# The last output projection of two attention layers, taken by token tiles instead of by weight pieces

## The chip, the cores and the metric

The kernel runs on one core of a Trainium2 chip. The engines of the core work side by side, each through its own instructions in order: TensorE (PE) multiplies matrices and transposes by multiplying with an identity, VectorE (DVE), ScalarE (ACT) and GpSimd (POOL) do the elementwise work, and SyncE (SP) issues the transfers (DMAs) between the chip's memory and the on-chip memory. The metric is the time of one execution in device microseconds (us), as the median of several runs.

## The reference

The model takes 512 tokens of width 1024. Two attention layers (the second one is a retention layer) are followed by a gated delta net and a mixture of experts. Cut to what matters here:

```python
def first_block(x, mem, norm_g, ..., w_out, final_norm_g):
    mem_n = rmsnorm(mem, mem_norm_g)
    for i in range(2):
        h = rmsnorm(x, norm_g[i])
        proj = h @ w_in[i]                     # q, k, v, q_mem, z
        main = fox_attention(...) if i == 0 else retention(...)   # 12 heads of 128
        memo = mem_cross_attention(q_mem, mem_n, w_mem_kv[i])     # 4 heads of 128
        o = concatenate([main, memo], -1) * silu(z)
        x = x + o @ w_out[i]                   # 2048 x 1024, the output projection
    return rmsnorm(x, final_norm_g)
...
# then: x -> rms_norm(x, mix_norm_g_2) @ w_in_2 -> short convolution + gated delta net (4 heads)
# beta = sigmoid(b), g = -exp(a_log) * softplus(a + dt_bias); b and a are 8 of the 3592 columns of w_in_2
# -> output projection, mixture of 32 experts
```

## The kernel before

Every matrix product is made in three matmuls, since each float32 operand is kept as a high and a low part (`wh`/`wl` for weights, `hH`/`hL` for the normalized tokens, `oh`/`ol` for an attention head's gated output). A weight piece is a DMA of 512 KB into a buffer `raw`; ACT writes `wh` from it (L201) and DVE writes `wl` = `raw` - `wh` (L202). There are two weight pools, each with its own `raw` and `wh`/`wl` buffers; `piece` (L187) takes them in a fixed rotation unless it is told a pool.

Tokens lie in four tiles of 128 (t = 0 to 3). A layer's output projection is made in three parts as the heads come; `out_proj` (L737) is called for the last six heads with `steps`, the parts of the normalization that follows. Its weight is cut in two column halves (nh) and three row pieces (kq), six pieces in all, and 4 x 6 x 6 = 144 matmuls of 128x512. Before the change each half goes piece by piece over all four tiles; only in the second half are the second and third piece kept, so that one tile after the other is finished. `add` (L753) puts each sum on the token rows `x`; `steps[0]` then does the squares, the product with the gain `gb` on POOL and, after the second half, the reciprocal square root and the scaling of the rows (`xs` in layer 1, `x` in layer 2). When all four tiles are finished, `steps[1]` transposes each tile on PE (8 transposes of 128x128, outputs `trp` or `att`) and ACT and DVE split the transposed tile into `hH` and `hL`. Only then can the next layer's projections run on that tile.

Layer 1 is followed by retention (`ret`): its first pair's projection goes tile by tile (`proj_tok`). Layer 2 is followed by the delta net (`dn`). It starts with `proj_few`, a narrow projection whose 8 columns `ba` give beta and the gate; it is made in two halves of 256 tokens, as are the k, q and v projections of head 0. From `ba` a chain runs over several engines: four small transposes on PE, a softplus and a running sum, a transfer out and back (`gd`, then `gb`, broadcast to all partitions), the decay `dtmp` and `E` on DVE, another pair of transfers (`lda`, `la`), a triangular inverse on DVE (`lx`), and its result goes into matmuls on PE through `XX`.

The instructions of each engine stand in an order which a scheduler made from the program text when the kernel was built; at run time each engine keeps that order and waits on semaphores. SP issues the DMAs in such an order too, so that a DMA that waits for a free buffer holds back the ones behind it.

## Time and profile before

| | |
|---|---|
| Time, median of 3 runs | 1806.19 us (1806.1 to 1808.04) |
| The profiled execution | 1808.52 us |
| Span from its first to its last instruction | 1806.7 us |
| PE busy | 1744.4 us, 97% |
| DVE, ACT, POOL busy | 56%, 32%, 8% |
| Mean granted PE clock | 0.991 of full speed |
| Last out_proj of layer 1 | its PE work begins at 523 us and ends at 559 us |
| Last out_proj of layer 2 | ends at 975 us |
| Delta net | from 986 us to about 1290 us |

Times inside the profile count from the span's start. A row of the timeline gives the start, the duration and, in brackets, how long the engine stood idle before it and what ended that. PE is pipelined: its rows overlap, and what a matmul costs is the distance to the next start. The table of stretches gives busy times and PEclk, the granted clock as a share of 2.4 GHz, so that 0.50 is 1.2 GHz.

### The profile page before, as it was taken

The page shows a single profiled execution, that of the slowest core. Times are in us where ns is not written, and L with a number is a line of the kernel's source. Part 1 is how long each engine was busy: PE and PEld are TensorE (multiplying, and loading weights), DVE is VectorE, ACT ScalarE, POOL GpSimd, SP SyncE. Part 2 cuts the span into 40 slices and gives each one's busy share as a digit, 9 for nine tenths or more (in the row PEclk, how much of TensorE's full clock was granted, in tenths as well). Part 3 has the DMA queues.
Part 4 walks back from the last instruction along what each step waited for, and adds up shares of the span by engine and source line. Part 5 has one row for each costly group of instructions (what it writes and reads, how often), then busy time and mean ns, then how long its engine had stood idle before and what let it go on. Part 6 is the DMA issues. An engine that isn't in the chain of part 4 may idle for free.

```text
span 1806.7 us, 25586 instructions
## 1 busy us (share of the span) xinstructions
PE 1744.4 (97%) x9945; PEld 1294.4 (72%) x9945; DVE 1016.6 (56%) x2557; ACT 576.8 (32%) x1082; POOL 146.7 (8%) x170
## 2 busy tenths in 40 slices
PE   6999999999998999999997999999999999999996
PEld 6888888878888998999876877778743544454443
DVE  7654563663756445454566788875454435444534
ACT  5543332443444232222344534434311111111112
POOL 1000000000004110111004000001200000000001
PEclk9999999999999999999998999999999999999998
DMA  7733233223232222223322243326699999999981
GB/s 235 198 95 90 76 93 94 82 82 94 59 120 86 82 71 82 83 72 92 90 77 56 78 98 83 89 66 243 265 422 390 408 406 422 407 411 408 420 332 48
DMA packets 199149, 320.94 MB, mean 178 GB/s; under 512 B 18189, under 2 KB 158950, under 8 KB 174322
## 3 DMA queue, kind: packets, MB, share of 16 engines
q1 hardware_dynamic: 199026, 319.28, 50.0%
q8 instruction: 79, 1.29, 0.3%
q14 instruction: 44, 0.36, 0.1%
HBM read 314.24 MB, written 5.01 MB: 177 GB/s over the span
## 4 chain that ended last, share of the span: by engine, by line
PE 86%; DVE 8%; DMA 2%; ACT 1%; issue 1%; POOL 0%; SPq 0%; POOLq 0%; DVEq 0%; ACTq 0%
PE acc L142 47%; PE pg L223 12%; PE att L142 7%; PE att L223 7%; PE pd L223 6%; PE trp L147 3%; PE trp L223 1%; PE trp L142 1%; DVE wl L202 1%; DVE rst L172 1%; DVE rsr L181 1%; DMA la<-lda 1%; DMA raw<-in_w_mem_kv_dram 0%; DVE on L1009 0%; DVE rss L1007 0%
## 5 line engine op out<-in xcount | busy, mean ns | idle before, releaser
L202 DVE TENSOR_TENSOR wl<-raw,wh 128x1024 fp32r<-128x1024 f32 x184 | 227.5, 1238 | 259.0 <-ACT wh L201 252.3
L201 ACT ACTIVATE wh<-raw 128x1024 fp32r<-128x1024 f32 x184 | 194.4, 1057 | 350.9 <-PE acc L142 327.9
L142 PE MATMUL acc<-hH,wh 128*128 128x512 f32 (+1 forms) x760 | 300.2, 396 | 0.0
L142 PE MATMUL acc<-hL,wh 128*128 128x512 f32 (+1 forms) x760 | 300.1, 395 | 0.0
L142 PE MATMUL acc<-hH,wl 128*128 128x512 f32 (+1 forms) x760 | 299.3, 394 | 0.0
L223 PE MATMUL pg<-mw,mhT 128*64 128x512 f32 x1024 | 230.3, 597 | 0.0
L142 PE MATMUL acc<-wh,hH 128*128 128x256 f32 x576 | 162.0, 281 | 4.2 <-ACT hH L236 4.2
L142 PEld LDWEIGHTS acc<-hH,wl 128*128 128x128 f32 x760 | 143.2, 188 | 27.3
L142 PEld LDWEIGHTS acc<-hH,wh 128*128 128x128 f32 x760 | 143.3, 189 | 26.9
L142 PEld LDWEIGHTS acc<-hL,wh 128*128 128x128 f32 x760 | 143.2, 188 | 26.7
L223 PEld LDWEIGHTS pg<-mw,mhT 128*64 128x64 f32 x1024 | 69.3, 137 | 129.8 <-issue 129.7
L142 PE MATMUL acc<-wh,hL 128*128 128x256 f32 x576 | 161.4, 280 | 0.0
L142 PE MATMUL acc<-wl,hH 128*128 128x256 f32 x576 | 161.3, 280 | 0.0
L142 PE MATMUL acc<-wh,oh 128*128 128x512 f32 x320 | 126.4, 395 | 1.4 <-ACT oh L236 1.4
L142 PE MATMUL acc<-wl,oh 128*128 128x512 f32 x320 | 126.0, 394 | 0.0
L142 PE MATMUL acc<-wh,ol 128*128 128x512 f32 x320 | 125.2, 392 | 0.0
L223 PE MATMUL pd<-mw,h 128*64 128x512 f32 (+1 forms) x544 | 118.3, 577 | 3.0 <-DVE h L1743 3.0
L142 PEld LDWEIGHTS acc<-wh,hH 128*128 128x128 f32 x576 | 108.6, 189 | 5.0 <-ACT hH L236 4.7
L142 PEld LDWEIGHTS acc<-wl,hH 128*128 128x128 f32 x576 | 108.7, 189 | 0.4
L142 PEld LDWEIGHTS acc<-wh,hL 128*128 128x128 f32 x576 | 108.5, 189 | 0.0
L1724 ACT ACTIVATE gu<-pg,gt 128x512 f32<-128x512 f32 x32 | 22.0, 688 | 267.0 <-PE pg L223 253.1
L1783 DVE TENSOR_TENSOR yl<-pd,yh 128x512 fp32r<-128x512 f32 x30 | 19.3, 686 | 137.3 <-ACT yh L1782 137.3
(536 smaller groups left out, 2900.0 us busy)
## 6 DMA issues: line engine op xcount, KB each, us to landing
mw<-in_w_gate_dram SPq DMA_DIRECT2D x64, 1024.0 KB, 10.7
mw<-in_w_up_dram SPq DMA_DIRECT2D x64, 1024.0 KB, 10.3
mw<-in_w_down_dram SPq DMA_DIRECT2D x62, 1024.0 KB, 10.5
raw<-in_fox_w_in_dram SPq DMA_DIRECT2D x56, 512.0 KB, 3.9
raw<-in_w_out_dram SPq DMA_DIRECT2D x40, 512.0 KB, 3.7
raw<-in_ret_w_in_dram SPq DMA_DIRECT2D x32, 512.0 KB, 3.9
raw<-in_w_in_dram SPq DMA_DIRECT2D x28, 512.0 KB, 4.0
raw<-in_w_mem_kv_dram SPq DMA_DIRECT2D x16, 512.0 KB, 8.5
```

Source lines behind the costliest of these rows:

```text
L142: self.pe.matmul(o, l, r, start=start, stop=stop)
L147: self.pe.transpose(o, i, self.ident[b:b + n, b:b + n])
L172: yield V.scalar_tensor_tensor(out=t, in0=r, scalar=w, in1=r, op0=ALU.mult, op1=ALU.mult)
L181: yield V.scalar_tensor_tensor(out=r, in0=t, scalar=c, in1=r, op0=ALU.subtract, op1=ALU.mult, reverse0=c == 768.0)
L201: nc.scalar.activation(h, raw, AF.Copy)
L202: nc.vector.tensor_tensor(l, raw, h.bitcast(F32), op=ALU.subtract)
L223: ins = getattr(eng, name)(*a, **k)
L1724: nc.scalar.activation(gu, pg.rearrange("p (n k) -> p k n", k=4), AF.Copy, scale=blk["us"][:, j:j + 1])
L1783: V.tensor_tensor(l, pd, h.bitcast(F32), op=ALU.subtract)
```

## The change

`out_proj` with `steps` now goes over the pieces only for the tiles 0 and 1 (both halves, with six sums), keeps all six split pieces, and then makes the tiles 2 and 3 one after the other, each with both halves at once. The transposes of tile 0 come after tile 2's sums, those of tiles 1 and 2 after tile 3's, and those of tile 3 are put into `self.pend`: the next layer calls them before the last tile's `proj_tok` of its first pair (ret), or in dn between the two halves of `proj_few`. dn makes the first halves of head 0's k, q and v projections there too, ahead of tile 3's transposes, and their second halves behind `proj_few`.

To keep six pieces, four more `wh`/`wl` pairs lie in a pool `wspx` that is opened for this call only, in space that the attention part frees. All six use the second pool's two `raw` buffers. Tile 3's normalized rows move to a buffer `xl` that outlives the call, and in layer 2 the last step on `x` is made for three tiles and then for the last one. retention's first pair takes its q and k pieces from the first weight pool.

```diff
-LASTP = (0, 1, 1)
+LASTP = ((1, 2, 2), (1, 2, 2))
+DNC = (("k", 2048), ("q", 1536), ("v", 2560))
...
+    def extra(self, stack):
+        self.wpools[2:] = [(self.wpools[1][0], self.pool("wspx", 4, stack=stack))]
...
     def out_proj(self, W, h0, heads, steps=None):
...
+        def add(t, nh, ps):
+            xv = self.x[:, t, nh * 512:(nh + 1) * 512]
+            nc.vector.tensor_tensor(xv, ps, xv, op=ALU.add)
+            if steps:
+                steps[0](t, nh)
+        w = [[], []]
         for nh in range(2):
-            pst = [self.acc() for _ in range(NT)]
-            w = []
-            last = nh and steps
-            c = 1 if last else nq
+            ts = range(2 if steps else NT)
+            pst = [self.acc() for _ in ts]
             for kq in range(nq):
-                w.append(self.piece(..., pool=LASTP[kq] if last else None))
-                if kq < c:
-                    for t in range(NT):
-                        mms(pst[t], t, kq, w[kq], kq == 0, kq == nq - 1)
-            for t in range(NT):
-                for kq in range(c, nq):
-                    mms(pst[t], t, kq, w[kq], False, kq == nq - 1)
-                xv = self.x[:, t, nh * 512:(nh + 1) * 512]
-                nc.vector.tensor_tensor(xv, pst[t], xv, op=ALU.add)
-                if steps:
-                    steps[0](t, nh)
-            if last:
-                for t in range(NT):
-                    steps[1](t)
+                w[nh].append(self.piece(..., pool=LASTP[nh][kq] if steps else None))
+                for t in ts:
+                    mms(pst[t], t, kq, w[nh][kq], kq == 0, kq == nq - 1)
+            for t in ts:
+                add(t, nh, pst[t])
+        if not steps:
+            return
+        for t in range(2, NT):
+            for nh in range(2):
+                ps = self.acc()
+                for kq in range(nq):
+                    mms(ps, t, kq, w[nh][kq], kq == 0, kq == nq - 1)
+                add(t, nh, ps)
+            steps[1](t - 2)
+        steps[1](2)
+        self.pend = lambda: steps[1](NT - 1)
...
# retention, pair 0
+                    if not pr and t == NT - 1:
+                        self.pend()
                     ps = self.acc()
                     self.proj_tok(ps[:, :256], wqk, self.hs, t)
...
# delta net
-        ps = self.proj_few(cp, Wr[:, :, 3488:3592], 96, 8, self.hs, cuts=2)
+        pre = {}
+        def first():
+            for n, c0 in DNC:
+                w = self.piece(Wr[:, :, c0:c0 + P])
+                pre[n] = (w, self.proj_T(w, self.hs, cut=0))
+            self.pend()
+        ps = self.proj_few(cp, Wr[:, :, 3488:3592], 96, 8, self.hs, cuts=2, between=first)
+        for n, (w, p) in pre.items():
+            self.proj_T(w, self.hs, ps=p, cut=1)
```

The order of three places, before and after. First SP's queue around the last out_proj of layer 1, before:

```order
L198 DMA raw<-in_w_out_dram 128x2x512 x6
L198 DMA raw<-in_ret_w_in_dram 128x4x128 x2
L198 DMA raw<-in_ret_w_in_dram 128x4x256
L198 DMA raw<-in_ret_w_in_dram 128x4x128 x2
L341 DMA gb<-in_norm_g_dram 128x1024
L897 DMA cr<-in_cr_dram 128x2708
```

and after:

```order
L199 DMA raw<-in_w_out_dram 128x2x512
L199 DMA raw<-in_ret_w_in_dram 128x4x128 x4
L199 DMA raw<-in_w_out_dram 128x2x512
L199 DMA raw<-in_ret_w_in_dram 128x4x256
L199 DMA raw<-in_w_out_dram 128x2x512
L199 DMA raw<-in_ret_w_in_dram 128x8x128
L199 DMA raw<-in_ret_w_in_dram 128x4x128 x2
L347 DMA gb<-in_norm_g_dram 128x1024
L916 DMA cr<-in_cr_dram 128x2708
L199 DMA raw<-in_w_out_dram 128x2x512 x3
```

The six pieces went in a row, ahead of the next layer's weights, the gain `gb` and the constants `cr`; now the last three stand behind all of these.

Second, PE at the last attention head of layer 1 (`att` is that head's output; `acc` are sums of out_proj; a `wh`/`wl` pair with neighbouring numbers is one piece), before:

```order
L142 MATMUL att_4854<-pT0h_4806,kvh_185 128x512
L142 MATMUL acc_4884<-wh_4887,oh_4212 128x512
L142 MATMUL acc_4884<-wl_4888,oh_4212 128x512
L142 MATMUL att_4854<-pT0l_4807,kvh_185 128x512
L142 MATMUL att_4854<-pT0h_4806,kvl_186 128x512
L142 MATMUL att_4854<-cb_4808,kvh_185 128x512
L142 MATMUL att_4854<-cb_4809,kvh_185 128x512
L142 MATMUL att_4854<-cb_4808,kvl_186 128x512
L142 MATMUL acc_4884<-wh_4887,ol_4213 128x512
```

and after:

```order
L148 MATMUL trp_4847<-ident_70,ms1_4834 128x128
L143 MATMUL att_4854<-pT0h_4806,kvh_185 128x512
L143 MATMUL att_4854<-pT0l_4807,kvh_185 128x512
L143 MATMUL att_4854<-pT0h_4806,kvl_186 128x512
L143 MATMUL att_4854<-cb_4808,kvh_185 128x512
L143 MATMUL att_4854<-cb_4809,kvh_185 128x512
L143 MATMUL att_4854<-cb_4808,kvl_186 128x512
L143 MATMUL acc_4884<-wh_4906,oh_4505 128x512
L143 MATMUL acc_4885<-wh_4906,oh_4505 128x512
L143 MATMUL acc_4884<-wl_4907,oh_4505 128x512
```

Twenty of the 144 matmuls stood around and among the last head's steps, before the end of its `att`; now twelve do, and the next ones read piece 2 (`wh_4906`), whose split stands on ACT and DVE behind the last head's `oh` and `ol`.

Third, PE in the delta net (`few` is the narrow projection's weight, `acc_9221` and `acc_9214` its sum, `acc_9309` and `acc_9399`, or `acc_9237`, `acc_9268` and `acc_9299`, those of k, q, v of head 0), before, where the transposes of `ba` stand 29 matmuls behind the last one of `few`:

```order
L142 MATMUL acc_9221<-hL_77,few_9216 32x256
L142 MATMUL acc_9221<-hH_76,few_9216 64x256
...
L142 MATMUL acc_9309<-hH_76,wl_9306 128x256
L147 MATMUL trp_9257<-ident_70,ba_9254 128x8 x4
L142 MATMUL acc_9399<-hL_77,wh_9395 128x256
```

and after:

```order
L143 MATMUL acc_9299<-hH_76,wl_9296 128x256
L148 MATMUL att_9324<-ident_70,x_71 128x128 x4
L148 MATMUL att_9331<-ident_70,x_71 128x128 x4
L143 MATMUL acc_9214<-hH_76,few_9209 64x256
...
L143 MATMUL acc_9214<-hH_76,few_9209 64x256
...
L143 MATMUL acc_9299<-hH_76,wl_9296 128x256
L148 MATMUL trp_9441<-ident_70,ba_9438 128x8 x4
L143 MATMUL acc_9670<-hH_76,wh_9666 128x512
```

Tile 3's transposes (`att_9324`, `att_9331`) now have the first halves of few, k, q and v ahead of them, and the transposes of `ba` have the second halves of k, q and v ahead of them, about 70 matmuls behind the last one of `few`.

## Rows read from the trace of the kernel before

**Rows 1.** Page, part 4: share of each engine in the chain.

```profile
PE 86%; DVE 8%; DMA 2%; ACT 1%; issue 1%; POOL 0%; SPq 0%; POOLq 0%; DVEq 0%; ACTq 0%
```

**Rows 2.** Stretches behind layer 1: busy PE, PEld, DVE, ACT, POOL, PEclk, DMA.

```profile
560.00:565.00 5.00, 1.75 (x10) 1.23 (x10) 4.68 (x15) 3.74 (x6) 2.33 (x2) 0.91 0.01 2
565.00:570.00 5.00, 3.18 (x15) 3.18 (x16) 5.00 (x14) 2.78 (x5) 0.00 (x0) 0.50 0.85 284
570.00:575.00 5.00, 5.00 (x41) 5.00 (x41) 2.00 (x8) 1.97 (x4) 0.00 (x0) 0.91 0.33 136
```

**Rows 3.** Timeline of PE there: start, us, instruction, [idle before <-releaser].

```profile
560.91 1.09 PE L147 MATMUL att<-ident,xs 128*128 128x128 f32 x8 [1.11 <-ACT xs L346]
563.92 0.45 PE L142 MATMUL acc<-wh,hH 128*128 128x256 f32 x1 [1.92 <-ACT hH L236]
566.82 0.58 PE L142 MATMUL acc<-wh,hH 128*128 128x256 f32 x1 [2.24 <-ACT hH L236]
```

**Rows 4.** The same table of stretches, behind layer 2.

```profile
980.00:985.00 5.00, 1.97 (x8) 1.57 (x8) 4.65 (x15) 3.13 (x7) 2.53 (x2) 0.55 0.01 2
985.00:990.00 5.00, 2.25 (x10) 1.99 (x11) 4.93 (x17) 2.43 (x6) 2.19 (x3) 0.50 0.36 105
990.00:995.00 5.00, 5.00 (x28) 4.66 (x27) 3.89 (x20) 1.90 (x3) 0.00 (x0) 0.58 0.01 3
```

**Rows 5.** Timeline of PE behind layer 2.

```profile
977.81 1.09 PE L147 MATMUL trp<-ident,x 128*128 128x128 f32 x8 [2.20 <-ACT x L346]
982.80 1.97 PE L147 MATMUL att<-ident,x 128*128 128x128 f32 x8 [3.89 <-ACT x L346]
986.37 0.44 PE L142 MATMUL acc<-hH,few 128*64 128x256 f32 x1 [1.60 <-POOL x L399]
988.84 1.97 PE L147 MATMUL trp<-ident,x 128*128 128x128 f32 x8 [1.39 <-ACT x L346]
```

**Rows 6.** Timeline of PE: out_proj of layer 1, its 21st and last matmul.

```profile
530.63 0.40 PE L142 MATMUL acc<-wh,ol 128*128 128x512 f32 x1
...
558.53 0.39 PE L142 MATMUL acc<-wh,ol 128*128 128x512 f32 x1
```

**Rows 7.** Page, part 5: the two halves of a split (busy, mean ns, idle before).

```profile
L202 DVE TENSOR_TENSOR wl<-raw,wh 128x1024 fp32r<-128x1024 f32 x184 | 227.5, 1238 | 259.0 <-ACT wh L201 252.3
L201 ACT ACTIVATE wh<-raw 128x1024 fp32r<-128x1024 f32 x184 | 194.4, 1057 | 350.9 <-PE acc L142 327.9
```

**Rows 8.** Timeline of DVE: the last head of layer 1.

```profile
532.22 0.69 DVE L240 SCALAR_TENSOR_TENSOR ol<-ot,oh 128x512 fp32r<-128x512 f32 x1 [0.70 <-ACT oh L236]
```

**Rows 9.** Page, part 6: DMA issues, KB each, median us to landing.

```profile
raw<-in_w_out_dram SPq DMA_DIRECT2D x40, 512.0 KB, 3.7
...
raw<-in_w_mem_kv_dram SPq DMA_DIRECT2D x16, 512.0 KB, 8.5
```

**Rows 10.** DMA issues from 526 to 545 us, the same columns.

```profile
cr<-in_cr_dram SPq DMA_DIRECT2D x1, 1354.0 KB, 5.9
```

**Rows 11.** Chain of work that ended last, layer 1's tile 0 (start, us, what).

```profile
550.80 0.70 DVE x L753
...
556.24 0.49 DVE xs L347
```

**Rows 12.** Timeline of DVE: a split before layer 2's last head.

```profile
939.72 3.05 DVE L202 TENSOR_TENSOR wl<-raw,wh 128x1024 fp32r<-128x1024 f32 x1
```

**Rows 13.** Timeline of DVE: tile 0's second sum in layer 2.

```profile
969.02 0.68 DVE L753 TENSOR_TENSOR x<-acc,x 128x512 f32<-128x512 f32 x1
```

**Rows 14.** Chain of work that ended last, start of the delta net.

```profile
1002.42 0.34 PE trp L147 x4
...
1012.60 3.95 DMA gb<-gd
...
1023.90 0.59 DVE dtmp L1220
```

**Rows 15.** Waits of PE from 1010 to 1290 us: sum, times, longest.

```profile
PE att L147 <- DVE cs L1203: 1.6, 1, 1.6
```

More of the change, by code (lines that the diff above doesn't have):

```diff
@@ L203, in piece, with halves @@
         return (h.rearrange("p (k n) -> p k n", k=k), l.rearrange("p (k n) -> p k n", k=k))
-    def halves(self, *srcs):
-        return [self.piece(*[a[:, c * 4:c * 4 + 4, :] for a in srcs]) for c in range(2)]
+    def halves(self, *srcs, pool=None):
+        return [self.piece(*[a[:, c * 4:c * 4 + 4, :] for a in srcs], pool=pool) for c in range(2)]
+    def extra(self, stack):
+        self.wpools[2:] = [(self.wpools[1][0], self.pool("wspx", 4, stack=stack))]
     def after(self, a, b):
@@ L266, in trp, with proj_T, proj_few @@
         return self.ptr.tile([P, 512], F32, tag="att", name="trp")
[L268 removed]
+    def proj_T(self, w, hs, n=S, m=P, ps=None, cut=None):
         H, L = w
         hH, hL = hs
[L272 removed]
+        ps = ps or self.acc()
         kd = H.shape[1]
[L274 to L279 removed]
+        sl = slice(0, n) if cut is None else slice(cut * n // 2, (cut + 1) * n // 2)
+        for k in range(kd):
+            self.mm(ps[:m, sl], H[:, k, :], hH[:, k, sl], k == 0, False)
+            self.mm(ps[:m, sl], H[:, k, :], hL[:, k, sl], False, False)
+            self.mm(ps[:m, sl], L[:, k, :], hH[:, k, sl], False, k == kd - 1)
         return ps
[L282 removed]
+    def proj_few(self, pool, src, c0, m, hs, cuts=1, between=None):
         nc = self.nc
@@ L300, in proj_few @@
                     self.mm(ps[:32, sl], w[:, k, 0:32], hL[:, k, sl], False, False)
+            if between and not c:
+                between()
         return ps
@@ L364, in norm_rows, with last_tile @@
         self.to_feat(xg, t, hs)
+    def last_tile(self):
+        return self.hp.tile([P, D], F32, tag="xl", name="xl")
     def norm_steps(self, pool, gb, hs):
         nc = self.nc
-        xg = [pool.tile([P, D], F32, tag=f"xs{t}", name="xs") for t in range(NT)]
+        xg = [pool.tile([P, D], F32, tag=f"xs{t}", name="xs") for t in range(NT - 1)] + [self.last_tile()]
         ss = [pool.tile([P, 2], F32, tag=f"ss{t}", name="ss") for t in range(NT)]
@@ L387, in norm2_steps @@
         V, G = nc.vector, nc.gpsimd
-        xg = [pool.tile([P, D], F32, tag=f"xs{t}", name="xs") for t in range(NT)]
+        xg = [pool.tile([P, D], F32, tag=f"xs{t}", name="xs") for t in range(NT - 1)] + [self.last_tile()]
         ss = [pool.tile([P, 2, 2], F32, tag=f"ss{t}", name="ss") for t in range(NT)]
-        s1 = pool.tile([P, NT], F32, tag="s1", name="s1")
+        s1 = self.sm.tile([P, NT], F32, tag="s1", bufs=1, name="s1")
         G.tensor_tensor(g2, g2, gf, op=ALU.mult)
@@ L409, in feat @@
             self.to_feat(self.x[:, t, :], t, hs)
-            if t == NT - 1:
-                r = self.rsqrt(self.sm, s1, "rx", 1.0 / D, EPS)
-                for u in range(NT):
-                    nc.scalar.activation(self.x[:, u, :], xg[u], AF.Copy, scale=r[:, u:u + 1])
+            if t >= NT - 2:
+                lo = 0 if t < NT - 1 else t
+                r = self.rsqrt(self.sm, s1[:, lo:t + 1], f"rx{t}", 1.0 / D, EPS)
+                for u in range(lo, t + 1):
+                    nc.scalar.activation(self.x[:, u, :], xg[u], AF.Copy, scale=r[:, u - lo:u - lo + 1])
         return step, feat
@@ L626, in fox @@
             xp = self.pool("xs1", 1, stack=sx)
+            self.extra(sx)
             self.out_proj(A["w_out"][0], PARTS[7][0], heads, self.norm_steps(xp, self.gain(xp, A["norm_g"][1:2, :]), self.hs))
+            self.wpools.pop()
     def ones_row(self, pool):
@@ L944, in ret @@
             xp = self.pool("xs2", 1, stack=sx)
+            self.extra(sx)
             gf = self.gain(xp, A["final_norm_g"][None, :])
@@ L1073, in dn @@
         mix = [None] * 8
-        gens = [self.dn_head(wk, h, Wr, C, sc) for h in range(4)]
+        gens = [self.dn_head(wk, h, Wr, C, sc, None if h else pre) for h in range(4)]
         po, sz = {}, {}
@@ L1169, in short_conv, with dn_head @@
         return self.split_a(self.op, o, "o", [P, S])
[L1171 removed]
+    def dn_head(self, wk, h, Wr, C, sc, pre):
         nc = self.nc
@@ L1194, in dn_head @@
         Kh, Qh, vb = T4("Kh", 2), T4("Qh", 2), T4("vb", 2)
-        for n, (nm, c0) in enumerate((("k", 2048), ("q", 1536), ("v", 2560))):
-            w = self.piece(Wr[:, :, c0 + h * P:c0 + (h + 1) * P])
-            ps = self.proj_T(w, self.hs, cuts=1 if h else 2)
+        for n, (nm, c0) in enumerate(DNC):
+            if pre:
+                ps = pre[nm][1]
+            else:
+                ps = self.proj_T(self.piece(Wr[:, :, c0 + h * P:c0 + (h + 1) * P]), self.hs)
             ci = {"q": 0, "k": 4, "v": 8}[nm] + h
```

17 lines of the change are left out of this document (4 added, 13 removed).

## The prediction

> **What bounds the kernel now.** I read the chain of waits first: 86% of the span lies on PE and 8% on DVE [rows 1], so time can come only from stretches in which PE stands or runs slowly. The table of stretches and PE's timeline then show where the change acts. Behind layer 1's out_proj PE waits three times for the normalized tiles, 1.11 + 1.92 + 2.24 = 5.27 us [rows 3], and the granted clock falls to 0.50, which is 1.2 GHz [rows 2]. The busy time there, weighted with what the clock lacks, is lost too: 1.75 x 0.09 + 3.18 x 0.50 + 5.00 x 0.09 = 2.2 us. Behind layer 2's it waits 2.20 + 3.89 + 1.60 + 1.39 = 9.1 us [rows 5], and 1.97 x 0.45 + 2.25 x 0.50 + 5.00 x 0.42 = 4.1 us go to the clock [rows 4]. So 7.5 us in layer 1 and 13.2 us in layer 2 are what there is to win, 20.7 us or 1.1%. Behind that the delta net keeps PE busy: its longest single wait from 1010 to 1290 us is 1.6 us [rows 15].
>
> **The change, layer 1.** No matmul is added or dropped: the sum is one of waits. An out_proj matmul costs (558.53 - 530.63) / 123 = 0.227 us [rows 6].
> *The tail's waits go.* Behind tile 0's sums there are now 31 matmuls of tile 2, 7.0 us, before its transposes; its normalization took 556.24 + 0.49 - 550.80 = 5.9 us [rows 11]. Tiles 1 and 2 have tile 3's 36 matmuls (8.2 us) over them, and tile 3 has the first three tiles' projections. So I take all 7.5 us as removed; if that cover falls, the 5.27 us come back.
> *Less cover at the last head.* Twelve matmuls instead of twenty stand before the end of its att: 8 x 0.227 = 1.8 us are still to be done. Its att ends earlier, since three of those stood between its own steps (3 x 0.227, about 0.65 us). Loss 1.15 us; att ends at about 529.95.
> *Piece 2 is late.* Its split stands behind the last head's oh and ol. ol ended at 532.91 [rows 8], so about 532.25 now; wh needs 1.06 and wl 1.24 us [rows 7]: wh from 531.5 to 532.5, wl from 532.5 to 533.75. PE waits 529.95 to 532.5 = 2.55 us, does two matmuls (0.45) and waits another 0.8 us for wl. Before, all six raws had been fetched long ahead, in one row on the queue.
> *Pieces 4 and 6 come in a ring.* All six use two raw buffers: DMA 4 waits for the split of piece 2 (533.75), DMA 6 for that of piece 4; and 4 stands on SP's queue behind gb and cr, which wait for the last head's end. A landing takes 3.7 us by its own kind and 8.5 us for the slowest raw of this kernel [rows 9]; cr, 1354 KB, took 5.9 [rows 10]. I take 5.0 for piece 4, which shares the engines with cr, and 3.7 for piece 6. Then piece 4 lands at 538.75, wh is there at 539.8, wl at 541.05. PE ends pieces 2 and 3 at 533.75 + 22 x 0.227 = 538.74 and waits 1.1 us for wh; six matmuls, four of them of tile 2 with piece 1, cover wl. Piece 6 lands at 544.75 and is split at 547.05; PE is there at 546.9 and waits 0.15 us. With 3.7 for both PE waits for neither; with 8.5 it waits 4.6 and another 4.8 us.
> *Sum of layer 1:* 7.5 - 1.15 - 2.55 - 0.8 - 1.1 - 0.15 = 1.75 us. The first wait is long enough that the clock may fall behind it (3.35 of 3.8 us idle; before the fall of rows 2 it was 5.27 of some 7). I take 1.0 us for layer 1.
>
> **Layer 2.** The same pieces, with two gain rows in front of DMA 4 instead of cr. Eight matmuls less at the last head cost 1.8 us again; but the split that took 3.05 us in front of that head's softmax [rows 12], and for which PE stood there, has moved away: 1.24 would be its normal time [rows 7] and all of it is gone from that place, of which 1.4 us lay on PE's path. Loss 0.4. Piece 2: 2.55 + 0.8, as above. Pieces 4 and 6 with 3.7 us, but with the sums and row scalings before their wl on DVE: 0.4 and 0.6. Tile 0's normalization takes 977.81 - 969.02 = 8.8 us here [rows 5, 13], against 7.0 us of cover and a sum that is made some 0.5 us late: 1.3 to 1.8, I take 1.3. Added 6.05 us, removed 13.2: gain 7.2 us. PE then comes to the end of head 0's k, q, v about 7 us earlier than before.
>
> A rule of the Trainium skill speaks for a higher price of those splits. Its page "SBUF — State Buffer", section "SBUF: two separate sides", says that DVE and GpSimd take turns at one port pair, for a whole instruction each; the trace agrees, with 3.05 us for a split beside POOL's product of the gains, 1.24 alone. By it a split of piece 4 or 6 that meets a product of a gain on POOL would be some 1.8 us late, and with one such meeting in each layer the total would be 3.6 us less.
>
> **What the delta net keeps.** The queue that pays is PE's order for ba: its transposes, at 1002.42 [rows 14], now stand behind the second halves of k, q and v, some 40 matmuls of 256 columns later, and come at about 1007, though few itself ends no later than before. The gate's broadcast landed at 1012.60 + 3.95 = 1016.55, 14.1 us behind the transposes [rows 14]; now at about 1021 to 1023. What waits for it first is dtmp, at 1023.90 [rows 14], and that was held by DVE's own queue (convolutions, splits), not by the gate. By DVE's new order that queue comes to dtmp at about 1023.5. So head 0's chain moves by less than 1 us, while PE is 8 us early. It does not stand, since the new order puts more projection work ahead of the first matmul that needs XX: counted from the order at the trace's spacings, 961.8 us of PE work instead of 952.6, 9.2 us more; 8.0, 5.0 and 5.2 us more before the points of heads 1 to 3. The lead of 8.2 us fits under the first and nearly under the second; at the third up to 3 us could be given back, unless that head's chain is earlier as well. I take 1 us. Behind the delta net the experts follow PE without a wait for weights, so that what is left there is left at the end.
>
> **Sum.** 1.0 + 7.2 - 1.0 = 7.2 us. Against the profiled execution that is 1808.52 - 7.2 = 1801.3; it lies 2.3 us above the median of the runs, so the forecast is 1806.19 - 7.2 = 1799.0 us.
>
> **Rivals.**
> *More: the pieces come in time.* If ACT and DVE do piece 2 earlier than I think (the waits of 3.35 us in each layer go) and nothing is given back in the delta net: 7.2 + 6.7 = 14, 1792. Against it stands the order, in which those splits are behind oh and ol.
> *Same (A): the gate decides.* If dtmp is held by the gate after all, with all of DVE's queue behind it, the chain of head 0 comes up to 6.5 us later, PE runs out of its 9.2 us of extra work, and about 6 us of the lead go: gain 1 to 2 us, 1804.7. For it: DVE and PE keep their orders, so what stands behind dtmp cannot pass it.
> *Same (C): the clock.* PE stands 3.35 us in short order at the start of both out_projs. If the clock falls there as it did behind the tails, 30 matmul places become 15 for some 7 us, the length of the stretch at 0.50 in rows 2: 3.4 us a layer, less what pieces 4 and 6 would have cost (1.25 and 1.0): 4.6 us together, gain 2.6 us, 1803.6. Against it: rows 2 and 4 show the fall only after more idle time. The Trainium skill's page "TensorE: Matmul & The Clock Gate", section "HAM oscillation — how this bites in real kernels", describes this very pattern, a loop that waits for a weight tile before each short burst and is cold in every one; by that rule C is the outcome, and it is why C has a chance of its own.
> *Slower (B): the ring.* Four transfers (pieces 4 and 6 of both layers) now lie between a split and PE, where none did. Each microsecond more of a landing is a microsecond of PE. At 8.5 us [rows 9] it is 4.6 + 4.8 - 1.25 = 8.2 us more in layer 1 and about as much in layer 2: 7.2 - 16.4 = -9, 1815. The gain is gone when each landing is 1.8 us longer than I took, and it is slower by 0.2% from 2.7 us, landings of 6.4 to 7.7 us. For it: cr's 5.9 us on the same queue. Against it: 40 transfers of w_out at a median of 3.7.
>
> **How the numbers follow.** 0.2% (3.6 us) is about what a measurement of this kernel can tell from no change. Chances: the forecast 0.50, more 0.10, A 0.16, C 0.11, B 0.13. Faster 0.60 (the forecast and more), same 0.27 (A and C), slower 0.13 (B). The forecast's own range: layer 1 from 0 to 3 us (both landing bounds near 3.7, or the clock), layer 2 from 5 to 8, the delta net from 0 to -3: gain 3.6 to 11, 1795 to 1802.6. A and C reach to 1804.7; a part of B with landings just over 6 us to 1807. So 1795 to 1807, which leaves out most of "more" and the larger part of B.
>
> **What would show it.** Right: no waits of 1 us or more before the transposes, and PEclk near 1.00 behind both out_projs; new waits of PE for wh and wl of piece 2, of 2 to 3 us, in both layers, and smaller ones at pieces 4 and 6; the last retention projection of the first pair about 1 us early, the end of head 0's k, q, v 7 to 8 us early, gd some 5 to 7 us late, and dtmp at an unchanged time. Wrong: landings of w_out over 6 us there, PEclk at 0.50 within the out_projs, or a wait of PE of several us for XX or for the rows of head 0.

## The result: slower by 0.63%, and the profile after

| | us, median | runs | profiled execution, span |
|---|---|---|---|
| before | 1807.12 | 4 | 1806.7 |
| after | 1818.87 (1817.48 to 1822.83) | 4 | 1821.0 |

The ratio of after to before is 1.0063, with an interval of 1.0048 to 1.0077: 11.4 us slower (1.0063 x 1807.12 - 1807.12), where 7.2 us faster was forecast. The time lies above the range.

The chain of the changed kernel reads as before: PE carries nearly all of it, against [rows 1] (page, part 4, share of the span by engine).

```profile
PE 87%; DVE 8%; DMA 2%; ACT 2%; issue 1%; POOL 0%; SPq 0%; POOLq 0%; ACTq 0%; DVEq 0%
```

So I read where PE stands. The table of stretches of after, around layer 1's out_proj (busy PE, PEld, DVE, ACT, POOL, then PEclk, DMA share, GB/s), answers [rows 2]:

```profile
530.00:540.00 10.00, 6.21 (x23) 3.69 (x23) 6.52 (x12) 4.41 (x9) 0.00 (x0) 0.92 0.20 60
540.00:550.00 10.00, 7.46 (x26) 5.61 (x25) 3.41 (x4) 3.34 (x6) 2.56 (x2) 0.84 0.48 184
550.00:560.00 10.00, 10.00 (x40) 8.01 (x40) 2.88 (x5) 1.78 (x3) 1.02 (x1) 0.90 0.57 160
560.00:570.00 10.00, 10.00 (x49) 8.22 (x48) 8.79 (x31) 5.66 (x11) 4.15 (x4) 1.00 0.00 1
```

Behind the out_proj PE is busy all the time and its granted clock is 1.00: the tail's waits are gone, as the change means. In front they have come back: 3.79 and 2.54 us of the first two rows are idle, and the clock lies at 0.92, 0.84 and 0.90, where the kernel before had 1.00 from 520 to 560 us, until its tail. PE's timeline of after in that stretch names the waits, against [rows 3] (start, us, instruction, idle before it and releaser):

```profile
532.78 0.49 PE L143 MATMUL att<-pT0h,kvh 128*128 128x512 f32 x1 [0.64 <-ACT pT0h L241]
...
537.34 0.73 PE L143 MATMUL acc<-wh,oh 128*128 128x512 f32 x2 [2.39 <-ACT wh L202]
538.60 0.79 PE L143 MATMUL acc<-wl,oh 128*128 128x512 f32 x1 [0.53 <-DVE wl L203]
539.19 0.63 PE L143 MATMUL acc<-wh,ol 128*128 128x512 f32 x1
539.62 0.63 PE L143 MATMUL acc<-wh,oh 128*128 128x512 f32 x1
...
542.25 0.39 PE L143 MATMUL acc<-wh,ol 128*128 128x512 f32 x1
542.48 0.40 PE L143 MATMUL acc<-wh,oh 128*128 128x512 f32 x1
...
547.99 1.12 PE L143 MATMUL acc<-wh,oh 128*128 128x512 f32 x3 [2.54 <-ACT wh L202]
```

2.39 and 0.53 us are piece 2, 2.54 us is piece 4. Between them the clock can be seen without the column PEclk: the matmuls behind 538.60 start 0.43 us apart (539.62 - 539.19), those behind 542.25 0.23 us (542.48 - 542.25). It is half, 1.2 GHz, for some 3.4 us, and again for as long behind 547.99. A fourth wait comes in the retention, 1.2 us, before `acc<-wh,hL` at 589.80.

Behind layer 2, against [rows 5], the same view:

```profile
954.98 0.41 PE L148 MATMUL trp<-ident,ms 128*128 128x128 f32 x2 [0.94 <-DVE ms L722]
...
961.49 1.11 PE L143 MATMUL acc<-wh,oh 128*128 128x512 f32 x2 [2.39 <-ACT wh L202]
...
988.07 1.09 PE L148 MATMUL trp<-ident,x 128*128 128x128 f32 x8 [1.28 <-ACT x L352]
...
1001.42 0.30 PE L143 MATMUL acc<-hH,few 128*64 128x256 f32 x1 [2.18 <-ACT hH L241]
```

and the stretches there, against [rows 4]: full clock around the old tail, 0.83 behind each of the two waits of over 2 us.

```profile
960.00:970.00 10.00, 8.36 (x29) 6.23 (x30) 4.53 (x6) 4.91 (x7) 1.33 (x2) 0.83 0.31 105
...
980.00:990.00 10.00, 8.72 (x43) 6.89 (x42) 8.50 (x23) 4.60 (x13) 7.46 (x6) 1.00 0.00 0
990.00:1000.00 10.00, 9.24 (x49) 7.57 (x47) 8.53 (x32) 5.56 (x11) 4.81 (x4) 1.00 0.15 16
1000.00:1010.00 10.00, 8.24 (x56) 7.84 (x57) 5.57 (x26) 6.76 (x14) 3.77 (x5) 0.83 0.27 80
```

In the delta net, where [rows 15] had 1.6 us as the longest wait, one of 3.2 us has come, before `acc<-hH,wh` and released by DVE's `sz`.

None of this explains all of it. From one run of projections to the last before out_proj, where the two kernels run the same instructions, before takes 432.87 - 52.85 = 380.0 us and after 437.07 - 55.62 = 381.5. The first experiment is about that.

### The profile page after: what moved, and what is told of

Read it like the earlier page. It is cut to its first block, busy times and chain, and to the rows that moved or that the text cites. A ratio compares the mean times of both kernels' runs of the same rounds, so it can differ in the third digit from the quotient of the medians.

```text
span 1821.0 us, 25591 instructions
## 1 busy us (share of the span) xinstructions
PE 1757.6 (97%) x9945; PEld 1303.4 (72%) x9945; DVE 1012.6 (56%) x2565; ACT 576.1 (32%) x1082; POOL 142.1 (8%) x170
## 4 chain that ended last, share of the span: by engine, by line
PE 87%; DVE 8%; DMA 2%; ACT 2%; issue 1%; POOL 0%; SPq 0%; POOLq 0%; ACTq 0%; DVEq 0%
PE acc L143 48%; PE pg L228 12%; PE att L143 7%; PE att L228 7%; PE pd L228 6%; PE trp L148 3%; PE trp L228 1%; PE trp L143 1%; DVE wl L203 1%; ACT wh L202 0%; PE att L148 0%; DVE on L1032 0%; DVE rss L1030 0%; DVE rst L173 0%; DMA mem<-in_mem_dram 0%
## 6 DMA issues: line engine op xcount, KB each, us to landing
mw<-in_w_gate_dram SPq DMA_DIRECT2D x64, 1024.0 KB, 10.6
```

## Experiment 1: the place of the buffers

The trace shows it in a run of 96 equal matmuls of layer 1 (first and last row of the run in PE's timeline). Before:

```profile
99.79 0.28 PE L142 MATMUL acc<-wh,hH 128*128 128x256 f32 x1
...
110.98 0.28 PE L142 MATMUL acc<-wh,hL 128*128 128x256 f32 x1
```

After:

```profile
102.67 0.28 PE L143 MATMUL acc<-wh,hH 128*128 128x256 f32 x1
...
114.08 0.28 PE L143 MATMUL acc<-wh,hL 128*128 128x256 f32 x1
```

(110.98 - 99.79) / 95 = 117.8 ns from start to start before, (114.08 - 102.67) / 95 = 120.1 ns after. The duration in each row, 0.28, says nothing of it; only the distance of the starts does. What differs for these matmuls is where an operand lies. The change moves the little tile `s1` into the pool `sm` and gives `rsqrt` tiles of its own there (`rx2`, `rx3`), and the pools that come behind `sm`, those of the weight pieces and of the head outputs among them, all start 288 bytes later. `hH` and `hL` stand at the other end of the memory (their pool is opened with `side="right"`) and do not move with `sm`; in after they lie 4096 bytes lower, to make room for `xl`. To tell that from the rest of the change, the kernel before got only the shift, a tile of 72 floats (288 bytes) that nothing reads. There `hH` and `hL` stay where they are, so that of the operands of these 96 matmuls the weight pieces alone lie elsewhere:

```diff
 self.sm = self.pool("sm", 2, stack=d2)
+nc.vector.memset(self.sm.tile([P, 72], F32, tag="pad", bufs=1, name="pad"), 0.0)
```

> The kernel before, with 288 bytes a partition of unused space put into the pool of small tiles, so that every weight buffer (wh, wl) starts 288 bytes later, as it does in the changed kernel. In the profile of the changed kernel the matmuls of 256 columns that read these buffers follow one another at 119 to 121 ns instead of 117.5 to 118.5, from the first layer on, before any changed code runs. Theory A (the place of the buffers sets that spacing): 119 to 121 ns here too, 1728 such matmuls in the token projections times 2 ns, 3 to 4 us slower than before. Rival (it is chance of that one execution, or something else of the changed program): 117.5 to 118.5 ns and no difference in time.

Measured: 1815.27 us, ratio 1.0034 (1.0021 to 1.0046), and 120.0 ns. So 288 bytes of nothing cost about 6 us, half of what the change lost. How the place counts was then asked with more sizes of the same tile, in the kernel before (b_) and in the changed one (a_). If 64 bytes had been the unit, 32 bytes more in after would have mended it:

> The changed kernel with 32 bytes more of such space, so that its weight buffers start 320 bytes later than before, a multiple of 64 as the difference to the place before. Theory A, with the place modulo 64 as what counts: spacing 117.5 to 118.5 ns again and 3 to 4 us faster than the changed kernel, about 1815. If another modulus counts, or the rival holds: as the changed kernel, 1818 to 1819.

Measured: 1816.24 us, 1.0045 (1.0032 to 1.0059), 120.0 ns in the same run of matmuls and 118.6 in some later ones. A unit of 64 bytes is out. 384 bytes in a variant of the changed kernel (a_two, below):

> The kernel with pieces 1 and 2 in the second weight pool (1807.1 us, 0.9995 of before), with 96 bytes a partition of unused space in the pool of small tiles, so that the weight buffers start 384 bytes behind their place before: the same place modulo 128, another one modulo 256. The shift of 288 alone cost the kernel before 0.34%, 6 us, and 320 was not better in spacing. Theory A, place modulo 128: the 256-column matmuls follow at 117.5 ns again, the clock does not fall at 46 us of the span, and the time is 5 to 7 us less, 1800 to 1802. Rival (another modulus, or the neighbourhood of other tiles): spacing 119 to 121 ns, 1806 to 1808.

Measured: 1797.37 us, 0.9936 (0.9918 to 0.9954), 9.8 us less than the variant without the tile, and more than expected: the run of 96 now takes 113.5 ns each, faster than in the kernel before. So this run of matmuls shows not two distances but at least three. 256 bytes in the kernel before, which keeps the place modulo 256:

> The kernel before with 256 bytes of unused space: the same place modulo 256 (and 128). Theory A, place modulo 128 or 256: spacing 117.5 ns and the time of the kernel before, within 1 us. Rival (any move away from the place before costs it): 119 to 121 ns and about 6 us slower, as with 288.

Measured: 1808.64 us, 0.9998 (0.9985 to 1.001), 117.8 ns: no change. 384 bytes, and then 128, which are the same modulo 256:

> The kernel before with 384 bytes of unused space: its weight buffers at the very addresses that the kernel with two pieces in the second pool and 96 bytes has (1797.4 us; there the 256-column matmuls followed at 115.7 ns and those of 512 columns at 230.0, before at 117.4 and 233.3). Theory A (the spacing goes with the place of the weight buffers alone): 115.7 and 230.0 ns here too, 1570 matmuls times 1.7 ns and 1510 times 3.3 ns, 7 to 8 us faster than before, 1800 to 1801. Rival (it needs the changed kernel's other tiles, hH moved by 4096 bytes among them): 117 and 233 ns, 1808.

> The kernel before with 128 bytes of unused space, to see by what distance the places repeat. Weight buffers at 32 bytes past a multiple of 256 gave 117.4 and 233.3 ns (before, and 256 bytes on), at 64 past 120 and 233.9, at 96 past 119.4 and 232.5, at 160 past (384 bytes on) 115.9 and 229.8. Here they lie at 160 past again. If the place repeats every 256 bytes: 115.9 and 229.8 ns, and the time of 384, 1801. If a longer distance counts: another spacing, and a time like before's 1808.

Measured: 1800.9 us, 0.9959 (0.9944 to 0.9974), and 1800.86 us, 0.9961 (0.9949 to 0.9973), both at 113.5 ns. The run of b_384:

```profile
99.99 0.28 PE L142 MATMUL acc<-wh,hH 128*128 128x256 f32 x1
...
110.77 0.28 PE L142 MATMUL acc<-wh,hL 128*128 128x256 f32 x1
```

And 96 bytes in the changed kernel as it is, 384 in all:

> The changed kernel, its pieces as in the change, at the same addresses of the weight buffers (96 bytes of unused space). Theory A: 8 to 10 us faster than the changed kernel, about 1809 to 1811, and against the kernel before at those addresses the change itself costs 8 to 10 us, the loss that the traces show in layer 1 (5.6 us) and in the delta net (3.2). Rival (the place matters less here than with two pieces in the second pool): 1816 and more.

Measured: 1808.2 us, 0.9994 (0.9982 to 1.0007), 113.5 ns. The place of the first split piece (`wh`) modulo 256 bytes is taken as the label. Layer 1 has six such runs of 96, and right behind each of them one of 24 matmuls with 512 columns, in which `hH` or `hL` is the operand that is loaded and the weight piece the one that moves through; the table has the mean distance of the starts in each:

| place of `wh` modulo 256 | kernels | six runs of 96, ns | six runs of 24, 512 columns, ns | kernel before here, us |
|---|---|---|---|---|
| 32 | before, b_256 | 117.8 in all | 233.3 | 1807 to 1809 |
| 64 | after, b_shift, a_two | 120.0 or 120.1 in all | 233.7 to 234.1 | 1815.3 |
| 96 | a_pad32 | 120.0 in three, 118.6 in three | 232.3 to 232.5 | not run |
| 160 | b_384, b_128, a_p96, a_two_p96, best | 113.5 or 113.6 in 25 of 30, 117.8 in five | 228.8 to 229.9 | 1800.9 |

The place does not settle every run. best and a_two_p96 have one program and one set of places in layer 1, and the second run of 96 in best is this:

```profile
154.35 0.28 PE L143 MATMUL acc<-wh,hH 128*128 128x256 f32 x1
...
165.54 0.28 PE L143 MATMUL acc<-wh,hL 128*128 128x256 f32 x1
```

That is (165.54 - 154.35) / 95 = 117.8 ns, where a_two_p96 has (165.13 - 154.34) / 95 = 113.6. Behind layer 1 both distances occur at place 32 as well: before itself has 113.9 ns in the run at 574.5 us and 118.2 in the one at 612.3. At 64 no long run in any of these traces is below 119.9. So the place goes with which distance is the usual one, and what picks it in a single run is open. The matmuls of out_proj, whose two operands both lie behind the added tile and move together, keep 226.7 to 226.9 ns over 124 starts in before, b_256, b_shift, b_384 and b_128. It may then be the distance between the two operands that counts and not the place itself; no run parts the two.

What the change costs by itself is then read at equal place: after against b_shift 3.6 us (1818.87 - 1815.27), a_p96 against b_384 7.3 us (1808.2 - 1800.9). By the ratios, each against the kernel before in its own set of runs, it is 5.2 ((1.0063 - 1.0034) x 1807) and 6.3 us ((0.9994 - 0.9959) x 1808). The spans of the profiled executions differ by 6.8 (1821.0 - 1814.2) and 6.2 us (1807.6 - 1801.4). So 4 to 7 us belong to what the change does, and 5 to 7 to where it put the buffers: b_shift's median is 6.9 us above before's in the same runs, its ratio says 6.1, and of the 7.5 us between the two spans 2.2 are there at the start of layer 1's projections (55.06 against 52.85), from a fall of the clock that the last section tells of, and 5.3 come behind it.

## Where the rest is: time lost by stage

With the place out of the way the stages can be compared. For the table I took from each trace the distances of the starts of consecutive matmuls, and summed over each stage what they exceed the usual (lower quartile) distance of the same two forms in the kernel where that is shortest; waits, clock and spacing are all in it. Stages run from the last head pair's projections in layer 1 (437 us in after) to the retention's (623), to the last of that (850), to the end of `few`, from which `ba` comes (1018), to the experts (1317), to the end.

| us lost | layer 1, its out_proj | retention | layer 2, its out_proj | delta net | experts |
|---|---|---|---|---|---|
| b_shift (place 64) | 17.5 | 11.6 | 22.7 | 36.0 | 300.0 |
| after (64) | 22.5 | 11.6 | 21.9 | 40.4 | 298.4 |
| a_two (64) | 12.7 | 11.7 | 18.0 | 40.4 | 298.5 |
| a_gate (64) | 12.8 | 11.6 | 18.2 | 37.3 | 298.2 |
| b_384 (160) | 15.2 | 9.6 | 22.8 | 35.4 | 299.9 |
| a_p96 (160) | 19.7 | 9.7 | 22.0 | 39.9 | 298.3 |
| best (160) | 10.6 | 8.9 | 12.7 | 37.2 | 299.8 |

After against b_shift: layer 1 loses 5.0 us, layer 2 wins 0.8, the delta net loses 4.4, the experts win 1.6. a_p96 against b_384 gives 4.5, 0.8, 4.5 and 1.6: nearly the same four numbers at another place. The first three stages were then changed one at a time, layer 2 and the delta net on top of the kernel of experiment 3.

## Experiment 2: layer 1 alone put back

Layer 1 gets its out_proj of before (all four tiles together), layer 2 and the delta net keep the change:

```diff
-self.out_proj(A["w_out"][0], ..., self.norm_steps(xp, ...))
+self.out_proj(A["w_out"][0], ..., self.norm_steps(xp, ...), old=True)
```

> The change in layer 2 and the delta net alone: layer 1's out_proj, its pools and its transposes are as before. By the traces the change cost layer 1 about 5.6 us (time lost between matmuls 14.6 us instead of 9.0) and won 1.7 us in layer 2, while the delta net lost 3.2. Theory W and A: 1818.9 - 5.6 = about 1813. Rival (layer 1's loss is made good later, since something else sets the end): no difference to the changed kernel, 1818 to 1819.

Measured: 1814.54 us, 1.004 (1.0026 to 1.0053), 4.3 us under after. The old tail is back with its lower clock (560 to 570 us of a_l2):

```profile
560.00:570.00 10.00, 4.66 (x27) 3.59 (x26) 9.55 (x26) 6.65 (x12) 3.60 (x2) 0.84 0.18 53
570.00:580.00 10.00, 10.00 (x73) 9.95 (x72) 6.74 (x20) 4.46 (x6) 1.13 (x2) 0.82 0.43 159
```

and still the kernel is faster: the change made layer 1 dearer than the tail that it removed, by about 4.3 us, as the stage's 5.0 says.

## Experiment 3: the pieces from a second pool

If the waits for wh are what costs, they must go when the split of piece 2 is made earlier. In after its pair of buffers lies in the added pool `wspx`, in space that the attention part frees with its last head. Here pieces 2 and 4 change places: piece 2 gets the free pair of the second pool, piece 4 one of the added pool.

```diff
-LASTP = ((1, 2, 2), (1, 2, 2))
+LASTP = ((1, 1, 2), (2, 2, 2))
```

(Row nh of the table, place kq: the pool of piece 3 nh + kq + 1. It holds for both layers.)

> The changed kernel with pieces 1 and 2 in the second weight pool and pieces 3 to 6 in the new one: piece 2 no longer waits for space that the attention part frees, and is split before the last head. Theory W (most of the loss in the two out_projs is piece 2's late split and the clock that falls behind that wait): in each layer the wait of 2.4 us for wh and 0.5 for wl goes, the first fall of the clock with it (1.8 us), and the last head has its cover back (0.9): 9 to 11 us faster than the changed kernel in all, 1808 to 1810. Piece 4 or 5 still stands behind the squares on ACT, so one wait of some 2 us may be left in layer 1. Rival (the ring of two raw buffers is the cost, not piece 2's place): the wait moves to piece 3 or 4 and the clock falls there, 0 to 3 us faster, 1816 to 1819.

Measured: 1807.14 us, 0.9995 (0.9986 to 1.0005), 11.7 us under after at the same place of the buffers, and 8.1 under b_shift. ACT's timeline in layer 1, first of a_two, where the split of piece 2 now stands ahead of the last head's oh:

```profile
525.37 1.05 ACT L202 ACTIVATE wh<-raw 128x1024 fp32r<-128x1024 f32 x1
...
534.13 0.63 ACT L241 ACTIVATE oh<-ot 128x512 fp32r<-128x512 f32 x1 [2.47 <-DVE ot L552]
534.67 1.99 ACT L202 ACTIVATE wh<-raw 128x1024 fp32r<-128x1024 f32 x2
```

and of after, where it comes behind it, with piece 3's:

```profile
535.71 0.63 ACT L241 ACTIVATE oh<-ot 128x512 fp32r<-128x512 f32 x1 [2.49 <-DVE ot L552]
536.24 1.99 ACT L202 ACTIVATE wh<-raw 128x1024 fp32r<-128x1024 f32 x2
```

The waits of PE in a_two, 528 to 606 us (sum, times, longest):

```profile
PE acc L143 <- ACT wh L202: 1.7, 2, 1.5
```

where after has 4.9 for wh, 0.5 for wl, 1.2 for hL, 0.6 for pT0h. And no fall of the clock is left (a_two, 530 to 550 us):

```profile
530.00:540.00 10.00, 8.32 (x37) 5.86 (x36) 6.02 (x9) 4.25 (x7) 0.54 (x1) 1.00 0.63 232
540.00:550.00 10.00, 10.00 (x44) 8.10 (x44) 3.54 (x4) 2.93 (x5) 4.26 (x3) 1.00 0.52 172
```

In after the fall stood behind the waits of 2.39 and 0.53 us; behind the 1.5 us that a_two keeps the clock stays at 1.00. The transfers are no faster here: each trace has the landing of one piece of w_out in this stretch, 6.3 us behind its issue in a_two and 6.5 in after, where [rows 9] has a median of 3.7 over all forty. But piece 4's transfer is issued at 528.67 in a_two and at 538.57 in after, since its buffer is free once piece 2 is split. So the edit took the ring's wait away together with piece 2's, and does not part the two. Layer 1 is 4.8 us better than b_shift now (17.5 to 12.7), where the prediction had looked for a gain of 1.0.

## Experiment 4: the wait before few

In layer 2 a_two has kept one wait, 3.1 us, for hH of the normalized tiles, the one that after has at 1001.42. ACT's timeline of after shows what stood ahead of that hH:

```profile
999.04 1.15 ACT L423 ACTIVATE x<-xs,rx2r 128x1024 f32<-128x1024 f32 x1 [0.59 <-DVE rx2r L182]
1000.09 0.61 ACT L343 ACTIVATE junk<-xl 128x512 bf16<-128x512 f32 x1
1000.61 0.19 ACT L343 ACTIVATION_READ_ACCUMULATOR junk<-xl 128x1 f32 x1
1000.71 0.57 ACT L241 ACTIVATE hH<-att 128x512 fp32r<-128x512 f32 x1
```

The transposes of tiles 1 and 2 come one behind the other right before few, and their splits queue on ACT behind a row scaling and a square. So, in a_two, the transposes of tile 1 were put between the halves of tile 3's sums, 18 matmuls ahead of those of tile 2:

```diff
+                if t == 3 and not nh:
+                    steps[1](1)
-            steps[1](t - 2)
+            if t == 2:
+                steps[1](0)
```

> The kernel with pieces 1 and 2 in the second weight pool, and tile 1's transposes between the two halves of tile 3's sums instead of behind both. In its trace PE waits 3.1 us in layer 2 for the high part of tile 1 right behind the transposes of tiles 1 and 2, since ACT stands in front of it with work on x, and the clock falls behind that wait (1.7 us). Theory (that wait is the last large one of layer 2, and the lead counts): the wait and the fall go, 3 to 5 us faster than 1807.1, about 1803. Rival (the delta net gives any lead back at its own waits): within 1 us.

Measured: 1804.03 us, 0.9975 (0.9963 to 0.9987), 3.1 us under a_two. Its waits from 935 to 1012 us no longer have hH on top:

```profile
PE acc L143 <- ACT wh L202: 2.2, 3, 1.5
PE acc L143 <- DVE hL L243: 1.3, 1, 1.3
PE acc L143 <- DVE wl L203: 0.8, 1, 0.8
```

## Experiment 5: the gate

In a_two again, of the second halves of k, q and v only k's stays ahead of the transposes of ba; those of q and v go behind:

```diff
-for n, (w, p) in pre.items():
-    self.proj_T(w, self.hs, ps=p, cut=1)
+late = list(pre.values())
+self.proj_T(late[0][0], self.hs, ps=late[0][1], cut=1)
 ...                       # transposes of ba
+for w, p in late[1:]:
+    self.proj_T(w, self.hs, ps=p, cut=1)
```

> The kernel with pieces 1 and 2 in the second weight pool, and in the delta net ba's transposes behind the second half of k alone, ahead of those of q and v, as before the change; nothing else is moved. Theory G (the later gate is what eats the lead in the delta net): ba's transposes come 5 us earlier, dtmp and E of head 0 some 2 to 3 us earlier, and the kernel is 2 to 5 us faster than 1807.1. Rival (DVE's own queue holds dtmp, and the lead is lost at another place, at 1170 us where PE waits 3.2 us for sz): within 1 us.

Measured: 1804.05 us, 0.9978 (0.9967 to 0.999), 3.1 us under a_two, and all of it in the delta net (40.4 to 37.3). The waits of a_two there, 1012 to 1300 us, begin with

```profile
PE acc L143 <- DVE sz L546: 3.2, 1, 3.2
```

and a_gate's with

```profile
PE att L143 <- DMA XX<-ldx: 2.0, 2, 1.1
```

The wait for sz, some 160 us behind ba's transposes (1010.2 to 1170.2 us in a_two), is gone with it. That wait also took the clock down, 0.83 from 1170 to 1180 us in a_two, which a_gate has at 1.00. Two theories had this step: that the gate's chain is late and its lateness travels through DVE's order to that place, and that the new order of the projections makes the wait whatever the gate does. DVE's timeline before that wait speaks for the second. In a_two:

```profile
1165.84 0.69 DVE L1255 TENSOR_TENSOR dtmp<-gb,Gc 128x512 f32<-128x512 f32 x1
...
1169.48 0.67 DVE L546 SCALAR_TENSOR_TENSOR sz<-th,acc 128x512 f32<-128x512 f32 x1
```

and in a_gate:

```profile
1165.23 0.68 DVE L1257 TENSOR_TENSOR dtmp<-gb,Gc 128x512 f32<-128x512 f32 x1
...
1165.90 0.69 DVE L546 SCALAR_TENSOR_TENSOR sz<-th,acc 128x512 f32<-128x512 f32 x1
```

In a_two, as in after, DVE's order has `vb`, `E` and `ET` between this head's `dtmp` and `sz`, which starts 3.64 us behind `dtmp`; in a_gate, as in b_shift, `sz` comes ahead of them, 0.67 us behind it. DVE had no work left over: in a_two it stood idle for 1.44 us at 1164.57, just before. And head 0's `dtmp` is only 0.9 us earlier in a_gate (1026.50 against 1027.43). So the traces put the wait down to where the scheduler set `sz` on DVE, which went with the place of q's and v's projections; that order of DVE was not tried by itself.

## Experiment 6: all together

The second pool, tile 1's transposes between the halves, the earlier gate, and 96 bytes:

> All that helped, together: two pieces in the second pool, tile 1's transposes between the halves of tile 3's sums, ba's transposes ahead of q's and v's second halves, and the 96 bytes. If the gains of 9.8, 3.1 and 3.1 us add up: 1791. If the waits that the two moves take away are one and the same lead (the delta net gives back what both win): 1794.

Measured: 1789.94 us, 0.9894 (0.9876 to 0.9912), 18.4 us under the kernel before in the same runs, and 11.0 under b_384, which has the same place. What each brought alone is roughly the sum: 11.7 (pool), 3.1, 3.1 and 9.8 to 10.7 (place) from 1818.87 make 1790.3 to 1791.2. The waits of PE in layer 2 are those of a_mid; in the delta net the longest group is

```profile
PE att L143 <- DMA XX<-ldx: 1.5, 2, 1.0
```

so that PE does wait for XX there, as the prediction had looked for, once it comes early enough.

## Why the prediction was wrong, point by point

The steps that failed, in us of the kernel: the place of the buffers was put at nothing and cost 5 to 7; the clock was priced at 0.75 in layer 1 and at nothing in layer 2, and its falls took 2.7 and 2.8; the wait before few was put at nothing and took 2.18; piece 4 in layer 1 was put at 1.1 and took 2.54; the delta net was to lose 1.0 and lost 4.4.

**A term that was not there: the place.** The prediction says "No matmul is added or dropped: the sum is one of waits". No matmul was, but each of some three thousand got slower with the place of the weight pieces, by about 2 ns for the 256-column ones and 0.4 to 0.8 for those of 512. That is 5 to 7 us, and no wait shows them. The diff had it: `s1` and two `rsqrt` tiles in a pool ahead of those of the weights.

**The tail's waits go: right.** All 7.5 us in layer 1 are gone; in layer 2 only tile 0's transposes wait, 1.28 us; and the clock behind both out_projs is 1.00, in layer 2 up to the wait before few. What was wrong is that tiles 1 to 3 were taken as covered at no cost. Their splits are later on ACT's and DVE's queues, and PE met them: 1.2 us for hL at 589.80 and 2.18 us for hH at 1001.42, with a fall of the clock behind the second. In layer 1 it is DVE's row that shows why: the split of the second layer's keys, which was ready late, went ahead of tile 3's.

```profile
586.12 2.29 DVE L243 TENSOR_TENSOR kvl<-kvf,kvh 128x2048 fp32r<-128x2048 f32 x1 [2.01 <-ACT kvh L241]
...
589.06 1.28 DVE L243 TENSOR_TENSOR hL<-att,hH 128x512 fp32r<-128x512 f32 x2
```

**Less cover at the last head:** 1.15 us predicted; the new waits for pT0h and pT0l there are 0.64 and 0.23.

**Piece 2: right.** 2.55 and 0.8 predicted, 2.39 and 0.53 measured in layer 1, 2.39 and 0.3 in layer 2.

**Piece 4: mis-sized in layer 1,** 1.1 us predicted and 2.54 measured. Two things stood ahead of its wh. The transfer whose landing the trace has, piece 5's, took 6.5 us, where 5.0 were taken for piece 4; and ACT had squares of the first sums in its order before it:

```profile
544.80 0.63 ACT L343 ACTIVATE junk<-x 128x512 bf16<-128x512 f32 x1 [6.57 <-DVE x L752]
...
546.27 0.63 ACT L343 ACTIVATE junk<-x 128x512 bf16<-128x512 f32 x1 [0.74 <-DVE x L752]
...
546.90 1.99 ACT L202 ACTIVATE wh<-raw 128x1024 fp32r<-128x1024 f32 x2
```

Piece 4 was issued at 538.57; with 6.5 us it lies there at 545.1, and ACT takes it at 546.90. By that 1.8 us are ACT's order and the rest the landing, but the trace gives no landing of this one transfer, so the split stays an estimate. Rival B (the ring) had priced just this wait, from landings alone; 6.5 us is the lower edge of what it called decisive. In layer 2 PE waits at no piece 4 or 6 for more than 0.3 us. The slow split beside POOL's product of a gain came once, at 971.0 us, with 2.32 us instead of 1.22, and PE did not have to wait for it.

**The clock: rival C, given 0.11, came in both layers.** It is in the text as a rival, and "the clock may fall behind it" cost 0.75 us in the sum. It took, in the way that the prediction counted [rows 2], 6.21 x 0.08 + 7.46 x 0.16 + 10.00 x 0.10 = 2.7 us in layer 1, as the second fall came behind piece 4 (by the distances of the starts, which leave the idle time out, some 3.1). The argument against it was that [rows 2, 4] show a fall only after more idle time; here 3.8 of some 6 us were idle before the first fall (0.64, 0.23, 2.39 and 0.53), and 2.54 in one piece before the second. The rule of the Trainium skill that the prediction named ("TensorE: Matmul & The Clock Gate", section "HAM oscillation — how this bites in real kernels") tells of a loop whose every step starts cold behind its wait for the next tile. These rows agree in that the work behind both waits for weights ran at the lower clock at its start; they differ in that the page's waits are for transfers and these for a split on ACT.

**Layer 2: 7.2 us forecast, 0.8 had** (22.7 to 21.9). Predicted right: piece 2, and tile 0's 1.3 us (1.28). Not predicted: 2.18 us before few, and two falls of the clock, 8.36 x 0.17 + 8.24 x 0.17 = 2.8 us. Those are 5.0 of the 6.4 us that lack.

**The delta net: 1.0 us forecast as lost, 4.4 lost.** What the prediction said of head 0 held: "that was held by DVE's own queue", and the later gate was free. In after gb's transfer, issued at 1039.46, landed 3.2 us later, and `dtmp` started at 1042.98 with no idle time of DVE before it. Counted from the last projections of layer 2 (844.5 us in b_shift, 850.0 in after) few's last matmul is 5.4 us later and `dtmp` 5.7, so that the gate added 0.3 and rival A is out. few is late by another step: it has the first halves of k, q and v ahead of it, and the lead of 7.2 us that was to cover them was 0.8, so that "few itself ends no later than before" failed with layer 2. In the delta net itself the step that failed is "at the third up to 3 us could be given back ... I take 1 us": the new order of DVE was followed up to head 0's `dtmp`, and waits were looked for at XX and at head 0's rows. It was a later head's `sz`, now behind `vb`, `E` and `ET` on DVE, that made PE wait 3.2 us, with a fall of the clock behind it (0.85 from 1180 to 1190 us in after).

**The experts** won 1.6 us that nothing had promised. The kernel before has a stretch at 0.85 and 0.81 there (1315 to 1325 us) that is missing in after. The change alone does not decide it: of the five traces of the kernel before and its padded forms four have such a fall between 1300 and 1330 us, and b_128 has none; of the nine with the change best alone has one, 0.66 from 1300 to 1305. What decides it is open.

By the stages at equal place, then: 5.0 us lost where 1.0 us of gain was forecast, 0.8 won for 7.2, 4.4 lost for 1.0, 1.6 won for 0; together 7.0 us lost for 7.2 won. The place comes on top with 5 to 7 us. That is 12 to 14 where the medians say 11.4, which is as closely as single executions tell it.

## What to carry to other kernels

Waits that are taken from the end of a loop by putting work there have been taken from somewhere, here from the start: before such a move, walk the new order of the split pieces through the queues that prepare them, and count the clock, which fell here behind the new waits as it had behind the old ones. A transpose that is moved behind other work still takes its slots on ACT and DVE, so look who stands behind it there, and follow the new order through to the later heads. And whenever an edit adds or moves even a small tile, compare the distance of the starts of equal matmuls in an untouched stretch before explaining anything else; if it moved, pad the kernel before by the same bytes and compare with that.

## What the runs showed of the hardware

The distance from start to start of back-to-back matmuls goes with where the weight pieces begin within 256 bytes: for 256 columns at the full clock it is mostly 113.5, 117.8 or 120.0 ns, the same program otherwise, worth 1800.9, 1808 and 1815.3 us in this kernel. 256 bytes more change nothing, 128 and 384 do the same. In the kernels b_256, b_shift, b_384 and b_128 `hH` and `hL` stayed in place, so it is the weight piece's place that changed the run of 96. It is not a rule for a single run: at the places 32 and 160 both 113.5 and 117.8 ns occur, in one program even (best and a_two_p96, layer 1). By what mechanism stays open. The Trainium skill's page "Advanced Engine Details and Errata", section "SBUF Cachelines", tells of 16-byte lines; all places compared here are multiples of 32 bytes apart, so that rule cannot tell them apart.

The clock can also be low in one execution and not in another where the instructions are the same. The same early stretch, in the profiled executions of before and of after:

```profile
45.00:55.00 10.00, 7.51 (x64) 7.32 (x65) 8.64 (x15) 8.20 (x15) 3.01 (x2) 1.00 0.64 163
```

```profile
45.00:55.00 10.00, 7.36 (x40) 7.36 (x41) 7.92 (x13) 7.58 (x12) 2.87 (x2) 0.66 0.67 166
```

Both kernels run the same instructions there. Of the fourteen traces that of before alone has no such fall from 40 to 55 us: b_384, a_p96 and a_two have 0.66 from 40 to 45, b_shift and b_128 from 45 to 55. Layer 1's projections begin at 52.85 us in before and at 53.4 to 55.6 in the others, so spans of single executions are compared from behind it.
